# A layer normalisation that streams through SBUF: four instead of three rows of the fourth tile loaded one by one on the ScalarE queue

## The chip, the cores and the metric

One core of one Trainium2 chip. The metric is the device time of one execution in microseconds (us), the median of several; lower is better. "Tile 3" is the fourth tile; tiles are counted from 0. A packet is what one of the core's 16 DMA engines moves at a time; in the traces a full tile is 128 packets of 32 KB, eight for each engine, and a single row 128 packets of 4 KB.

## The reference

```python
def setup_inputs():
    batch, seq, dim = 32, 512, 1024
    return {"x": np.random.randn(batch, seq, dim).astype(np.float32), "eps": 1e-5}

def reference(x, eps):
    mean = np.mean(x, axis=-1, keepdims=True)
    var = np.var(x, axis=-1, keepdims=True)
    return ((x - mean) / np.sqrt(var + eps)).astype(np.float32)
```

67.1 MB come in and 67.1 MB go out; nothing is reused.

## The kernel before

The 16384 rows are 17 tiles: 15 of 128x8 rows, one of 128x6 and one of 128x2. A ring of 48 rows per partition holds six tiles. The loads go out on the SyncE queue: six tiles at once, and then tile t+6 when the store of tile t has landed. VectorE takes the statistics, GpSimd combines them, ScalarE takes the root, normalises in place and issues the store. So the ScalarE queue holds the stores, and, ahead of them, the few row loads that the change is about.

```python
TILES = (8,) * 15 + (6, 2)
SLOT, SLOTS = 8, 6
HALVES = (4, 4)                       # tile 0 is loaded in two halves
EARLY, AHEAD = 3, 3                   # <- the change
# ...
    for k in range(AHEAD):            # rows 0..AHEAD-1 of tile 3, one DMA each
        load(nc.scalar, EARLY, k, 1, ahead)
    owner = {}
    for t, (K, row, at) in enumerate(plan):
        # ... waits for the stores that free the ring's rows
        if t == 0:
            load(nc.sync, t, 0, HALVES[0], landed[t])
            load(nc.sync, t, HALVES[0], HALVES[1], second)
            continue
        first = AHEAD if t == EARLY else 0
        dma = load(nc.sync, t, first, K - first, landed[t])
# ...
    def vector(t, arrived, turn):
        K, row, at = plan[t]
        if t == EARLY:
            nc.vector.wait_ge(ahead, 16 * AHEAD)
        statistics(at, K, landed[t], arrived)
        nc.vector.reciprocal(out=rstd[:, at : at + K], in_=std[:, at : at + K]
        )._wait_ge(rooted[t], turn).then_inc(inverse, 1)
# ... ScalarE, for each tile: the root, then each row, then the store
        for k in range(at, at + n):
            a = nc.scalar.activation(out=ring[:, k, :], in_=ring[:, k, :],
                func=AF.Identity, bias=nmr[:, k : k + 1], scale=rstd[:, k : k + 1],
            ).then_inc(act, 1)
            # ...
            nc.scalar.dma_start(out=rows_of(o2, row, K), in_=ring[:, at : at + K, :]
            )._wait_ge(act, row + K).then_inc(stored[t], 16)
```

Of the kernel before, what the change touches and what calls it, by code (L numbers as in the profile page):

```python
# [16 lines left out]
HALVES = (4, 4)  # L17


EARLY, AHEAD = 3, 3  # L20


@with_exitstack
# [270 lines left out]
```

## Time and profile before

| | before |
|---|---|
| time, median of 3 (lowest to highest) | 318.32 us (318.27 to 318.82) |
| span in the profile | 316.7 us |
| busy: VectorE, ScalarE, GpSimd | 50%, 48%, 14% |
| DMA engines | 90% or more in 38 of 40 slices |
| rate in the middle (90 to 265 us) | 433 GB/s |

The prediction shows the lines that carry this (in the timeline: start, length, engine, line, what). In the timeline of the kernel before (start, length, engine, line, what), the SyncE queue issues tile 7's load as soon as store 1 has landed, and VectorE starts as soon as tile 4 has:

```profile
72.90 19.70 SPq L102 DMA_DIRECT2D ring<-in_x_dram  x2
73.74 9.59 DVE L128 BATCH_NORM_STATS2 stats<-ring 128x6 f32<-128x512 f32 x16 [6.32 <-DMA ring<-in_x_dram]
...
305.72 0.34 ACTq L251 DMA_DIRECT2D out_dram<-ring  x1
```

Two merged issues stand in the first line; its start, 72.90, is the landing of store 1 to within a tenth of a us. The second says that tile 4 had landed at 73.74. The third is the issue of the last store.

### The profile page before, as it was taken

What the parts mean: (1) busy time and instruction counts of PE and PEld (TensorE: products, weight loads), DVE (VectorE), ACT (ScalarE), POOL (GpSimd) and SP (SyncE); (2) the same over time, 40 slices, a digit from 0 to 9 for tenths busy, and PEclk for the clock granted to TensorE, in tenths of its full rate; (3) what the DMA queues carried; (4) which work ended last, traced back from release to release, by engine and by line L of the source; (5) the groups of instructions that cost most, each with busy time, mean ns of one, the idle gap of its engine ahead of it and who ended that gap; (6) DMA issues with size and microseconds to landing.
All of it is one profiled execution on the core that took longest, in us unless ns stands there. A gap on an engine that the chain in (4) does not pass through costs nothing.

```text
span 316.7 us, 712 instructions
## 1 busy us (share of the span) xinstructions
DVE 157.0 (50%) x274; ACT 153.3 (48%) x147; POOL 43.6 (14%) x186
## 2 busy tenths in 40 slices
DVE  0656584916529074380934709256191652918300
ACT  1065094947091561907429083380924709156740
POOL 0151202020200202001020110202002020021300
DMA  7999999999999999999999999999999999999996
GB/s 288 440 447 414 397 430 430 445 418 447 426 439 423 439 435 430 439 430 435 426 435 430 447 414 447 426 439 435 435 426 435 426 435 435 444 412 429 449 419 261
DMA packets 5476, 134.25 MB, mean 424 GB/s; under 512 B 608, under 2 KB 608, under 8 KB 992
## 3 DMA queue, kind: packets, MB, share of 16 engines
q10 hardware_dynamic: 2880, 68.68, 50.4%
q1 hardware_dynamic: 2592, 65.54, 48.5%
q14 instruction: 4, 0.03, 0.0%
HBM read 67.11 MB, written 67.11 MB: 424 GB/s over the span
## 4 chain that ended last, share of the span: by engine, by line
DVE 43%; another core or an unknown queue 23%; DMA 12%; POOL 10%; ACT 4%; issue 4%; SPq 0%; ACTq 0%; DVEq 0%
DVE stats L128 42%; DMA ring<-in_x_dram 12%; ACT ring L240 3%; ACT std L232 1%; POOL dev L193 1%; POOL dev L198 1%; POOL dev L186 1%; POOL nmean L182 1%; POOL dev L191 1%; POOL half L176 1%; POOL half L199 1%; POOL nmean L180 1%; POOL ss L202 1%; DVE rstd L141 1%
## 5 line engine op out<-in xcount | busy, mean ns | idle before, releaser
L128 DVE BATCH_NORM_STATS2 stats<-ring 128x6 f32<-128x512 f32 x256 | 153.7, 678 | 92.7 <-DMA ring<-in_x_dram 92.7
L240 ACT ACTIVATE ring<-ring,nmr,rstd 128x1024 f32<-128x1024 f32 x128 | 146.8, 1226 | 11.7 <-POOL nmr L223 11.7
L232 ACT ACTIVATE std<-ss,eps_t 128x8 f32<-128x8 f32 (+3 forms) x18 | 5.4, 299 | 138.4 <-POOL ss L202 138.0
L176 POOL TENSOR_TENSOR half<-stats 128x16 f32<-128x16 f32 (+3 forms) x18 | 4.1, 230 | 235.4 <-DVE stats L128 235.4
L141 DVE RECIPROCAL rstd<-std 128x8 f32<-128x8 f32 (+2 forms) x16 | 3.2, 200 | 52.3 <-ACT std L232 52.3
L193 POOL TENSOR_SCALAR dev<-dev 128x32 f32<-128x32 f32 (+3 forms) x18 | 5.1, 281 | 1.6
L223 POOL TENSOR_TENSOR nmr<-nmean,rstd 128x8 f32<-128x8 f32 (+3 forms) x18 | 3.7, 205 | 11.4 <-DVE rstd L141 11.3
L198 POOL TENSOR_TENSOR dev<-dev,stats 128x32 f32<-128x32 f32 (+3 forms) x18 | 4.5, 252 | 1.5
L182 POOL TENSOR_SCALAR nmean<-nmean 128x8 f32<-128x8 f32 (+3 forms) x18 | 4.3, 238 | 1.6
L186 POOL TENSOR_TENSOR dev<-stats,nmean 128x32 f32<-128x32 f32 (+3 forms) x18 | 4.3, 238 | 1.5
L191 POOL TENSOR_TENSOR dev<-dev 128x32 f32<-128x32 f32 (+3 forms) x18 | 4.2, 235 | 1.4
L199 POOL TENSOR_TENSOR half<-dev 128x16 f32<-128x16 f32 (+3 forms) x18 | 3.8, 213 | 1.4
L180 POOL TENSOR_TENSOR nmean<-half 128x8 f32<-128x8 f32 (+3 forms) x18 | 3.6, 203 | 1.4
L202 POOL TENSOR_TENSOR ss<-half 128x8 f32<-128x8 f32 (+3 forms) x18 | 3.6, 202 | 1.4
L232 ACT ACT_TABLE_LOAD x1 | 1.3, 1283 | 2.3 <-issue 2.3
L212 POOL TENSOR_TENSOR rstd<-std,power 128x4 f32<-128x4 f32 x2 | 2.1, 1040 | 0.9 <-ACT std L232 0.9
L145 DVE MEMSET eps_t<- 128x1 f32 x1 | 0.1, 59 | 1.0 <-SPq L56 1.0
L275 POOL MEMSET const-float32-0.0<- 128x1 f32 x1 | 0.1, 99 | 0.2 <-issue 0.2
L275 POOL MEMSET const-uint8-127<- 128x1 uint8 x1 | 0.1, 103 | 0.0
L275 POOL MEMSET const-bfloat16-1.0<- 128x1 bf16 x1 | 0.1, 102 | 0.0
L275 POOL MEMSET const-float32-1.0<- 128x1 f32 x1 | 0.1, 99 | 0.0
L146 DVE MEMSET power<- 128x8 f32 x1 | 0.1, 65 | 0.0
## 6 DMA issues: line engine op xcount, KB each, us to landing
out_dram<-ring ACTq DMA_DIRECT2D x15, 4096.0 KB, 34.6
ring<-in_x_dram SPq DMA_DIRECT2D x13, 4096.0 KB, 58.9
ring<-in_x_dram SPq DMA_DIRECT2D x2, 2048.0 KB, 11.4
ring<-in_x_dram SPq DMA_DIRECT2D x1, 3072.0 KB, 56.5
out_dram<-ring ACTq DMA_DIRECT2D x1, 3072.0 KB, 10.3
ring<-in_x_dram SPq DMA_DIRECT2D x1, 2560.0 KB, 51.5
ring<-in_x_dram ACTq DMA_DIRECT2D x3, 512.0 KB, 14.5
ring<-in_x_dram SPq DMA_DIRECT2D x1, 1024.0 KB, 68.3
```

Of the source, the lines that this page charges most:

```text
L128: i = nc.vector.bn_stats(out=stats[:, k, s, :], in_=ring[:, k, s * BN_MAX : (s + 1) * BN_MAX],)
L176: g.tensor_tensor(out=h, in0=mean4[:, :, 0:2], in1=mean4[:, :, 2:4], op=ALU.add),
L180: n = gp(g.tensor_tensor(out=nm, in0=h[:, :, 0], in1=h[:, :, 1], op=ALU.add), *n)
L182: g.tensor_scalar(out=nm, in0=nm, scalar1=-1.0 / H, scalar2=None, op0=ALU.mult),
L186: g.tensor_tensor(out=d, in0=mean4, in1=nm.unsqueeze(2).to_broadcast([P, K, H]), op=ALU.add),
L191: n = gp(g.tensor_mul(out=d, in0=d, in1=d), *n)
L193: g.tensor_scalar(out=d, in0=d, scalar1=float(D // H), scalar2=None, op0=ALU.mult),
L198: n = gp(g.tensor_tensor(out=d, in0=d, in1=m2, op=ALU.add), *n)
L199: n = gp(g.tensor_tensor(out=h, in0=d[:, :, 0:2], in1=d[:, :, 2:4], op=ALU.add), *n)
L202: g.tensor_tensor(out=ss[:, at : at + K], in0=h[:, :, 0], in1=h[:, :, 1], op=ALU.add),
L232: nc.scalar.activation(out=std[:, at : at + n], in_=ss[:, at : at + n], func=AF.Sqrt, bias=eps_t[:], scale=1.0 / D,)._wait_ge(*summed[i]). ...
L240: a = nc.scalar.activation(out=ring[:, k, :], in_=ring[:, k, :], func=AF.Identity, bias=nmr[:, k : k + 1], scale=rstd[:, k : k + 1],).then ...
```

## The change

```diff
-EARLY, AHEAD = 3, 3
+EARLY, AHEAD = 3, 4
```

One more of tile 3's rows goes on the ScalarE queue at the start, in a DMA by itself, and one less in tile 3's load on the SyncE queue. The intent that the code suggests: to keep both queues busy until the first store is ready. Nothing else changes.

## The prediction

> **What bounds the kernel now.** I read the page's digits by slice first, then a table of stretches, then the timeline of the first 55 us and of the end, and at last the packet records of the trace (start, queue, size of each packet), counted by me where a view has only a sum. The page's two DMA lines:
>
> ```profile
> DMA  7999999999999999999999999999999999999996
> GB/s 288 440 447 414 397 430 430 445 418 447 426 439 423 439 435 430 439 430 435 426 435 430 447 414 447 426 439 435 435 426 435 426 435 435 444 412 429 449 419 261
> ```
>
> In 38 of the 40 slices the DMA engines are busy for 90% or more, while VectorE and ScalarE are busy for 50% and 48% of the span. The stretches (length, VectorE, ScalarE and GpSimd busy us with instruction counts, clock, DMA share, GB/s):
>
> ```profile
> 2.00:15.00 13.00, 4.84 (x8) 1.28 (x1) 0.47 (x3) 1.00 1.02 420
> 15.00:26.00 11.00, 4.85 (x8) 6.14 (x7) 5.92 (x20) 1.00 1.01 432
> 26.00:40.00 14.00, 9.79 (x17) 3.96 (x6) 2.35 (x10) 1.00 0.99 400
> 90.00:265.00 175.00, 88.15 (x153) 85.86 (x83) 21.00 (x90) 1.00 1.00 433
> 303.00:310.00 7.00, 0.01 (x1) 2.37 (x2) 0.20 (x1) 1.00 0.99 425
> 310.00:314.40 4.40, 0.00 (x0) 0.00 (x0) 0.00 (x0) 1.00 0.81 344
> 314.40:316.70 2.30, 0.00 (x0) 0.00 (x0) 0.00 (x0) 1.00 0.01 4
> ```
>
> From 2 us to 314.4 us the transfers never pause. At 433 GB/s the 134.22 MB read and written (67.11 each way, from the page) take 310.0 us. Add 2.0 us ahead of the first byte, 2.3 us after the last, and the stretches below 433: 0.4 us in 2 to 15 (13 x 13/433), 1.1 us in 26 to 40 (14 x 33/433), 0.9 us in 310 to 314.4 (4.4 x 89/433). That is 316.7 us, the span. The time reported is 1.7 us longer (318.44 us for the profiled execution). So the kernel is a constant amount of traffic at a constant rate. The chain of waits puts 42% on VectorE's statistics, but this is not the bound: each of them starts when a tile lands, and in between VectorE waits for DMA (92.7 us in all).
>
> The start, where the change sits:
>
> ```profile
> 0.90 1.39 ACTq L102 DMA_DIRECT2D ring<-in_x_dram  x3
> 9.44 4.84 DVE L128 BATCH_NORM_STATS2 stats<-ring 128x6 f32<-128x512 f32 x8 [8.33 <-DMA ring<-in_x_dram]
> 15.63 4.85 DVE L128 BATCH_NORM_STATS2 stats<-ring 128x6 f32<-128x512 f32 x8 [1.35 <-DMA ring<-in_x_dram]
> 26.60 9.59 DVE L128 BATCH_NORM_STATS2 stats<-ring 128x6 f32<-128x512 f32 x16 [6.12 <-DMA ring<-in_x_dram]
> 29.64 0.35 ACTq L251 DMA_DIRECT2D out_dram<-ring  x1
> 39.42 0.20 DVE L141 RECIPROCAL rstd<-std 128x8 f32<-128x8 f32 x1 [3.24 <-ACT std L232]
> 40.44 9.59 DVE L128 BATCH_NORM_STATS2 stats<-ring 128x6 f32<-128x512 f32 x16 [0.81 <-DMA ring<-in_x_dram]
> 54.39 0.70 DVE L128 BATCH_NORM_STATS2 stats<-ring 128x6 f32<-128x512 f32 x1 [0.93 <-DMA ring<-in_x_dram]
> ```
>
> The statistics start when tile 0's halves land (9.44, 15.63), then tile 1 (26.60), tile 2 (40.44), tile 3 (54.39). Tile 3 is the "fourth tile". The first store goes out at 29.64.
>
> **What the Trainium skill says.** First, "DMA: Bandwidth & Descriptors", section "Queues, rings and completion order": each DMA engine takes turns between the queues that have work, a packet at a time, and takes the descriptors of one queue in order. The packet records agree: each of tile 0's halves is 128 packets of 16 KB on the SyncE queue, and in the same time exactly one row's 128 packets of 4 KB go on the ScalarE queue (first row 2.8 to 9.0 us, second 9.2 to 15.1); the third goes beside tile 1's 128 packets of 32 KB (16.0 to 26.1). Second, same page, "Issuing engines are not separate DMA queues": both queues feed the same 16 engines, so a second queue saves issue time only. The trace agrees: by packet records it is 430.7 GB/s with both queues loading (15 to 26 us), 432.4 with the SyncE queue alone (26.5 to 30) and 433 with loads beside stores (90 to 265). Third, same page, "Where 436 GB/s comes from", gives a ceiling of 435.2 GB/s; 433 is next to it, so I expect no rate above it. Fourth, same page, "Why a DMA increments its semaphore by 16 and not by 1": transfers that share a semaphore are only known to have landed at the full count. The kernel waits for 16 times the number of rows, which becomes 64, so the change is sound.
>
> **The change part by part.**
> 1. Added: one row load on the ScalarE queue. Three take 1.39 us to issue from 0.90, so a fourth takes some 0.46 us. It delays ScalarE's table load (2.3 us) to about 2.8 us; ScalarE is first needed at 17.0 us. Off the path: 0.
> 2. Removed: one row from tile 3's load on the SyncE queue, 2.5 MB to 2.0 MB (20 KB packets become 16 KB). The bytes are the same in all: 0. The row's 128 packets of 4 KB move at about 159 ns each against 1213 ns for 32 KB: 25.8 against 27.0 GB/s an engine. Half a MB at 4% less is 0.05 us.
> 3. Moved: the fourth row comes after the third in the ScalarE queue, so it starts at 26 us, beside tile 2. The two halves and tile 1 land as before. Tile 2 is now 8 rounds per engine of 1.213 + 0.159 us = 11.0 us from about 25.8 us: its packets end near 36.8 us and it lands near 37.5. In the kernel before, it had the engines alone only until the first store's packets came at 33.7 us, and landed at 40.4.
> 4. The first store, issued at 29.64 as before, sits behind the fourth row in the same queue: its packets start near 36.8 us instead of 33.7. It then goes beside tile 3: 8 rounds of 1.213 + 0.627 us (32 KB and 16 KB) = 14.7 us, both done near 51.6 us. Before, the store's packets ended at 50.5 and tile 3's at 53.1. The store loses 1 us, tile 3 gains 1.5 us.
> 5. From there nothing is left. Store 1 depends on tile 1, which has not moved: issued at 49.1 us, first packet at 52.8 us in the kernel before, after a gap from 50.5 in which its queue was empty. The 1 us that store 0 loses falls into this gap. Tile 4 starts near 51.7 instead of 52.0, and store 1 at 52.8 as before, packet by packet beside it. So the loads are about 0.3 us ahead from there to the end, and the stores where they were.
> 6. VectorE: tile 2's statistics cannot start before the reciprocal of tile 1 is through (39.42 + 0.20), so they start at 39.6 instead of 40.4; tile 3's near 52.8 instead of 54.4. Both off the path.
> Sum: 0 issue, +0.05 packets, 0 total bytes, 0 to -0.3 at the loads' end, which doesn't shorten the traffic. The time stays 318.3 us.
>
> **The end.** Could earlier loads still help there? The last store is issued at 305.7 us and its first packet goes at 311.1, behind the store before it; that one is issued at 302.1 and moves from 303.7, right behind its own predecessor. So the stores left over cover the last tiles' computing, and the engines run to 314.4 us. A last tile that comes 0.3 us earlier waits longer in the queue.
>
> **The rivals.**
> (a) The dip at the first store goes. By packet records the rate is 285 to 290 GB/s in 32 to 34 us and under 420 in 34 to 36, which loses (2 x 146 + 46 + 16)/433 = 0.8 us; some load packets there take 1.8 to 2.2 us instead of 1.2. If it comes from the first store meeting a queue that was empty, a fourth row ahead of it may hide it: 317.5 us. For it: the dip sits right between issue (29.6) and first packet (33.7). Against: the first store has to come at some time; I expect the dip to move, at the same size.
> (b) Holding the stores back costs at the end: if all stores stayed 3 us late, the last 4 MB would end later, up to 321 us. Against: the engines never idle, so a late store is an early load, and the gap after store 0 takes up the delay.
> (c) The fourth row delays what the first statistics wait for: if the rows shared bandwidth in equal parts and not by turns, both halves would land up to 1.2 us later (0.52 MB at 433 GB/s). This would delay the first store by as much, and the traffic would go on: 318.3 us all the same.
> (d) The end has no room: store 15's first packet goes right behind store 14's last, so if the loads' end came later by x, the end would come later by up to x. I expect it earlier; at most +0.5 us, 318.8.
>
> **Range and chances.** The three runs lie within 0.55 us. The rivals that I can size reach from -0.8 to +0.5 us. The range for 8 in 10 is 317.6 to 319.1 us. Two per cent are 6.4 us; neither direction has a mechanism of that size while the engines run without a pause: 0.01 faster, 0.98 same, 0.01 slower.
>
> **What would show each step.** In the profile after: statistics at 9.4, 15.6 and 26.6 us as before (step 3); tile 2's at 39.6, released by the reciprocal and not by a load (3, 6); tile 3's near 52.8 (4); the first store issued at 29.6, its first packet near 36.8 (4); tile 4's statistics within 0.5 us of the 73.7 us of before, and the last store's issue within 0.5 us of 305.7 (5); 433 GB/s in 90 to 265 us and the traffic's end at 314.4. The prediction is wrong if the engines pause anywhere between 3 and 310 us, or if the rate in the middle changes: 1% of it is 3.1 us.

## The result, and the profile after

Ratios below are the mean time of one kernel's runs over that of the other's in the same rounds, so they are not quite the ratio of the medians quoted.

| | before | after |
|---|---|---|
| time, median (lowest to highest), 4 runs each | 318.56 (318.27 to 318.82) | 318.96 (318.71 to 319.04) |
| ratio, 95% interval | | 1.0011 (0.9994 to 1.0029) |
| repeated, 11 and 5 runs | 318.69 | 318.99; 1.0014 (1.0001 to 1.0027) |

The same time, if anything 0.3 to 0.4 us longer. The page's DMA lines of the changed kernel:

```profile
DMA  7999999999999999999999999999999999999995
GB/s 282 446 447 443 343 447 438 428 430 455 409 455 406 451 409 451 422 447 430 430 455 409 451 409 451 418 443 422 447 430 430 451 414 430 447 414 434 443 434 245
```

As full as before; only the weak slice has become one with 343 (31.7 to 39.6 us), where the kernel before had 397, after 414 in the slice ahead of it. The stretches, as in the prediction:

```profile
90.00:265.00 175.00, 88.16 (x153) 85.98 (x82) 20.99 (x90) 1.00 1.00 433
...
303.00:310.00 7.00, 0.00 (x0) 1.92 (x2) 0.00 (x0) 1.00 1.02 440
310.00:314.40 4.40, 0.00 (x0) 0.00 (x0) 0.00 (x0) 1.00 0.82 348
314.40:316.90 2.50, 0.00 (x0) 0.00 (x0) 0.00 (x0) 1.00 0.02 7
```

The middle has the same 433 GB/s, and the traffic ends where it did. The start and the end of the timeline after:

```profile
0.90 2.14 ACTq L102 DMA_DIRECT2D ring<-in_x_dram  x4
...
9.56 4.84 DVE L128 BATCH_NORM_STATS2 stats<-ring 128x6 f32<-128x512 f32 x8 [8.45 <-DMA ring<-in_x_dram]
15.73 4.85 DVE L128 BATCH_NORM_STATS2 stats<-ring 128x6 f32<-128x512 f32 x8 [1.33 <-DMA ring<-in_x_dram]
...
26.74 9.59 DVE L128 BATCH_NORM_STATS2 stats<-ring 128x6 f32<-128x512 f32 x16 [6.16 <-DMA ring<-in_x_dram]
29.77 0.35 ACTq L251 DMA_DIRECT2D out_dram<-ring  x1
39.57 0.20 DVE L141 RECIPROCAL rstd<-std 128x8 f32<-128x8 f32 x1 [3.24 <-ACT std L232]
39.69 9.54 DVE L128 BATCH_NORM_STATS2 stats<-ring 128x6 f32<-128x512 f32 x16
...
53.32 9.59 DVE L128 BATCH_NORM_STATS2 stats<-ring 128x6 f32<-128x512 f32 x16 [0.65 <-DMA ring<-in_x_dram]
...
304.95 0.34 ACTq L251 DMA_DIRECT2D out_dram<-ring  x1
```

Tile 0's halves and tile 1 come 0.1 us later, which is nothing. Tile 2's statistics start at 39.69 without a wait for a load behind them: the reciprocal held them. Tile 3's start at 53.32, 1.1 us earlier than before, and the last store is issued 0.8 us earlier. By the packet records the fourth row moves from 27.0 to 37.6 us, beside tile 2, and the first store's first packet goes at 38.3 us, where it went at 33.7. Not all of these differences need come from the change: the section on the lag returns to this.

### The profile page after: what moved, and what is told of

Its sections match the earlier page's. It is cut to its first block, busy times and chain, and to the rows that moved or that the text cites. A ratio compares the mean times of both kernels' runs of the same rounds, so it can differ in the third digit from the quotient of the medians.

```text
span 316.9 us, 713 instructions
## 1 busy us (share of the span) xinstructions
DVE 156.8 (49%) x274; ACT 153.3 (48%) x147; POOL 43.6 (14%) x186
## 4 chain that ended last, share of the span: by engine, by line
DVE 46%; another core or an unknown queue 23%; POOL 11%; DMA 8%; ACT 4%; issue 4%; SPq 0%; ACTq 0%; DVEq 0%
DVE stats L128 45%; DMA ring<-in_x_dram 8%; ACT ring L240 3%; ACT std L232 2%; POOL dev L193 1%; POOL dev L198 1%; POOL dev L186 1%; POOL nmean L182 1%; POOL dev L191 1%; POOL half L176 1%; POOL half L199 1%; POOL nmean L180 1%; POOL ss L202 1%; DVE rstd L141 1%
```

## The experiments

The prediction held, so the question was whether for its reasons. The theory: a constant amount of traffic at a constant rate, so that only pauses and a changed rate count, and a store that comes late is a load that comes early. Twelve runs are each of five rounds against the kernel before. One is the changed kernel again (the last line of the table above; 0 to 0.4 us slower was expected), and two have one execution more or less than five. Where packets are counted, it is from the packet records of the trace.

### No row ahead, and seven

```diff
-EARLY, AHEAD = 3, 4
+EARLY, AHEAD = 3, 0      # ahead0; and VectorE's wait for `ahead` only if AHEAD
+EARLY, AHEAD = 3, 7      # ahead7
```

> No row of tile 3 ahead; all on the SyncE queue. Theory (a constant amount of traffic without a pause): same time, 318.3 to 318.9 us; tile 0's halves land some 1.2 us earlier each (statistics near 8.3 and 13.3 us), tile 1 near 23, the first store is issued near 26.5; the dip of the rate sits at the first store, with the same size of 0.8 to 0.9 us. Rival 'each row ahead costs 0.15 to 0.3 us of the start': 317.7 to 318.1 us. Rival (d), no room at the end: the loads end up to 1 us later than with four rows, and the time is up to 0.5 us longer than before's.

Measured: 318.29 us (318.20 to 319.11), ratio to before 0.9992 (0.9978 to 1.0006). The statistics of the halves ran from 8.18 to 17.89 us without a gap, the second half having landed at 13.0. The first store was issued at 28.37 us, later than the 26.5 expected, which had followed the second half: ScalarE normalises the first half until 22.0 us and only then takes the second's root, so the issue goes by the first half, which came 1.3 us earlier than in the kernel before (8.18 and 9.44; 28.37 and 29.64). The loads' end and the last store (305.81 us) were where the kernel before had them.

> Seven rows of tile 3 ahead, on the ScalarE queue in front of the first store. By turns, a row goes beside each of tiles 1 to 5, so the first store's packets come after all six tiles' loads, near 61 us (38 with four rows), and tile 3's statistics start near 61 us (53 with four). Theory: a late store is an early load, the engines never pause, 318.4 to 319.5 us; the loads end tens of us before the end. Rival (b), a store held back is paid at the end: up to 23 us more, 330 to 342 us. Rival 'each row costs 0.15 to 0.3 us': 319.3 to 320.2 us.

Measured: 318.55 us (318.50 to 318.76), ratio 0.9993 (0.9979 to 1.0006). Tile 3, the middle and the last store's issue in this run:

```profile
63.41 9.59 DVE L128 BATCH_NORM_STATS2 stats<-ring 128x6 f32<-128x512 f32 x16 [10.74 <-DMA ring<-in_x_dram]
...
290.00 0.34 ACTq L251 DMA_DIRECT2D out_dram<-ring  x1
```

```profile
90.00:265.00 175.00, 96.95 (x169) 94.28 (x91) 23.15 (x100) 1.00 1.00 433
```

The first store's packets started at 61.3 us, 27.6 us later than in the kernel before, and it cost nothing: the loads had its place, the computing was over at 290 us, and the stores left over kept the engines at 433 GB/s. Rival (b) of the prediction, that a store held back is paid at the end, falls. The idea that each row costs 0.15 to 0.3 us finds no support: four rows more than in the kernel before would be 0.6 to 1.2 us, some 0.5 us was saved elsewhere (the dip, next), and the run was 0.2 us faster, with an interval from 0.7 us faster to 0.2 us slower. Only the low end of that price, some 0.1 us net, would still hide in this noise.

These runs also answer rival (a), on the dip at the first store. From 27 us to 72 us, the loss against 431 GB/s summed by half microseconds is 0.7 to 0.9 us in three profiles of the kernel before (two of them with additions at the end, see below), 1.0 to 1.2 in four of the changed one, 1.2 with no row ahead; with seven rows, where tile 5's load was just over when the first store began, it is 0.4 us, all of it thinly spread. The dip lies at 29.5 to 34 us with no row ahead, at 31.5 to 35.5 with three and at 35.5 to 39 with four, where the first store's packets start at 32.7, 33.7 and 38.3: it moves with the first store, as predicted, and begins 2 to 3 us ahead of its packets. It all but goes in the one run where that store meets no load. When tile 6's load then joined the running stores, at 76.7 us, nothing was lost (0.0 us from 72 to 100). Why it begins ahead of the packets, no run tells.

### The fourth row elsewhere

```diff
-    for k in range(AHEAD):            # row_sync: the first three only, and
+    for k in range(AHEAD - 1):
         load(nc.scalar, EARLY, k, 1, ahead)
# ... in the loop over the tiles:
+        if t == EARLY:                # ahead of tile 3's rest, on SyncE
+            load(nc.sync, EARLY, AHEAD - 1, 1, ahead)
```

> The fourth row is a load by itself, but on the SyncE queue right ahead of the rest of tile 3. Theory: what moved tile 2 and the first store is the place in the ScalarE queue alone: tile 2 lands at 40.4 and the first store's packets start near 33.7 us, as in the kernel before; 318.5 us. Rival: the split into one more transfer moves them: tile 2 at 37.4 and the first store near 38, as with four rows on the ScalarE queue.

Measured: 318.73 us (318.69 to 318.84), ratio 1.0000 (0.9986 to 1.0013). Tile 2's statistics started at 40.42 us, behind a load, and the first store's packets at 33.74, as in the kernel before:

```profile
40.42 9.59 DVE L130 BATCH_NORM_STATS2 stats<-ring 128x6 f32<-128x512 f32 x16 [0.70 <-DMA ring<-in_x_dram]
```

It is the place in the ScalarE queue that moves both, not the split.

```diff
+    load(nc.gpsimd, EARLY, AHEAD - 1, 1, fourth)   # row_gpsimd: a third queue
-    for k in range(AHEAD):
+    for k in range(AHEAD - 1):
         load(nc.scalar, EARLY, k, 1, ahead)
```

VectorE waits for the new semaphore too.

> The fourth row on GpSimd's queue, a third one. By turns of a packet it goes beside the first half: both halves and tile 1 land 1.2 us later than in the kernel before (statistics near 10.7, 16.9, 27.8 us), and so does the first store's issue, near 30.9. Theory: 318.5 us all the same. Rival: what delays the first statistics delays the end: 319.7 us.

Measured: 323.19 us (323.04 to 323.91), ratio 1.0143 (1.0126 to 1.0160). The arrivals came as expected, and the time did not:

```profile
10.53 4.84 DVE L130 BATCH_NORM_STATS2 stats<-ring 128x6 f32<-128x512 f32 x8 [9.41 <-DMA ring<-in_x_dram]
17.18 4.84 DVE L130 BATCH_NORM_STATS2 stats<-ring 128x6 f32<-128x512 f32 x8 [1.81 <-DMA ring<-in_x_dram]
28.01 9.59 DVE L130 BATCH_NORM_STATS2 stats<-ring 128x6 f32<-128x512 f32 x16 [5.99 <-DMA ring<-in_x_dram]
```

```profile
90.00:265.00 175.00, 88.15 (x153) 82.14 (x79) 20.83 (x90) 1.00 1.00 426
```

The halves and tile 1 are 1.1 to 1.6 us late, but the price is 4.5 us. Most of it is paid in the middle: 426 GB/s instead of 433, with the engines busy throughout (share 1.00), is 2.8 us in this stretch alone. Both theories of this run fail: the traffic is constant, its rate is not. In the packet records, around the end of every tile, load packets take up to 2.2 us instead of 1.213; 166 load packets between 60 and 265 us take over 1.3 us, where the kernel before has 1. And the 16 engines drift apart: the last store's 16 completions are spread over 3.9 us instead of 1.1.

### A tiny first store

```diff
             load(nc.sync, t, HALVES[0], HALVES[1], second)
+            nc.sync.dma_start(out=rows_of(o2, row, K)[:, 0, 0:SLOT], in_=power[:]
+            )._wait_ge(filled, 1).then_inc(warm, 16)
```

ScalarE waits for `warm` ahead of store 0, which writes the same bytes over.

> The changed kernel with a tiny first store (32 bytes in each of 128 partitions, written over later) on the SyncE queue behind tile 0's halves. If the dip of the rate belongs to the very first store of the program: it moves to about 15 us, and if its size goes with the store's, it all but goes, for 0.5 to 0.9 us less than the changed kernel. If it belongs to the first large store beside loads: the rate dips at 35 to 39 us as in the changed kernel, same time.

Measured: one run of 325.10 us, which is the profiled one; the other five, 330 to 337 us, are over 1.5% above it, and are not compared. Their granted clock is 1.00 like that of all others, so they may as well be this kernel's own times; only the 325.10 was profiled. The fast run alone: 1.020 against 318.69; there is no interval for it, and the time rests on one run. The dip stayed (a loss of 0.7 us from 27 to 72 us), and the middle was as in the run above: 425 GB/s, 143 slow load packets, a spread of 3.9 us at the end. Nothing was gained, but it showed the same slow middle without GpSimd's queue. What both had in common: store 1 was issued late (50.5 and 50.7 us, where the kernel before had 49.1), because tile 1 was, and its first packet came 2.4 us after that of tile 4's load. In all other kernels so far, with seven rows left aside, this lag was between 0 and 1.2 us. A load packet takes 1.213 us, so it is two load packets per engine against one or none.

### The lag by itself

```diff
+        if t == 1:                    # lag_store1, in the changed kernel
+            nc.scalar.activation(out=idle[:], in_=eps_t[:].to_broadcast([P, 1536]),
+                func=AF.Identity)._wait_ge(*summed[i])
```

> The changed kernel with one more ScalarE activation of 128x1536 (about 1.4 us) ahead of tile 1's normalising, so that store 1 is issued at 50.7 instead of 49.3 us and its packets follow tile 4's loads by 2.4 us (two load packets per engine) instead of 1.2 (one). In the run with the fourth row on GpSimd's queue and in the one with a tiny store this lag was 2.4 us, load packets took up to 2 us around every tile's end and the 16 engines drifted apart by 4 to 5 us. Theory 'it is the lag': the same here, 321 to 325 us. Rival 'it is the kind of the added transfer': 318.7 to 319.3 us, no slow packets in the middle. The first theory of a constant traffic at a constant rate says 319 us too.

Measured: 323.43 us (323.35 to 325.11), ratio 1.0155 (1.0138 to 1.0172). The issue of tile 7's load (store 1 landed), tile 4's statistics (tile 4 landed), and then the stretches:

```profile
74.73 20.92 SPq L103 DMA_DIRECT2D ring<-in_x_dram  x2
...
72.13 9.59 DVE L129 BATCH_NORM_STATS2 stats<-ring 128x6 f32<-128x512 f32 x16 [4.37 <-DMA ring<-in_x_dram]
```

```profile
90.00:265.00 175.00, 88.14 (x153) 81.71 (x79) 20.83 (x90) 1.00 1.00 425
...
303.00:310.00 7.00, 0.63 (x2) 6.08 (x7) 2.06 (x10) 1.00 0.92 396
```

Compare with the lines of before: there store 1 landed 0.8 us ahead of tile 4, here 2.6 us behind it. One activation of 1.48 us on ScalarE, some 280 us ahead of the end and with no transfer added, costs 4.4 us against the changed kernel (318.99). The rate is 425 GB/s in the middle, 142 load packets are slow, and at 303 to 310 us the engines' share is 0.92: by my reading some have run out of work, waiting for the last two stores (issued at 306.66 and 310.25), while others have not. The expectation's "4 to 5 us" of drift was too high: by the completions it is 3.9 in all three runs.

```diff
+        if i == 1:                    # gps_later: issued after the second half's work
+            load(nc.gpsimd, EARLY, AHEAD - 1, 1, fourth)
```

> The fourth row on GpSimd's queue again, but issued after the second half's GpSimd work, near 25 us, so that it goes beside tile 2 and leaves tile 0, tile 1 and the issue of store 1 (49.2 us) where they were in the kernel before; store 1's packets should follow tile 4's loads by 0.8 to 1.2 us. Theory 'it is the lag': 318.5 to 319.2 us. Rival 'a transfer on GpSimd's queue by itself makes the later packets slow': 322 to 324 us as in the earlier run.

Measured: 318.75 us (318.28 to 319.02), ratio 0.9996 (0.9981 to 1.0010). The same row on the same GpSimd queue, and this is its middle:

```profile
73.42 19.68 SPq L102 DMA_DIRECT2D ring<-in_x_dram  x2
...
74.43 9.59 DVE L129 BATCH_NORM_STATS2 stats<-ring 128x6 f32<-128x512 f32 x16 [6.24 <-DMA ring<-in_x_dram]
```

```profile
90.00:265.00 175.00, 88.13 (x153) 85.88 (x83) 20.82 (x90) 1.00 1.00 432
```

GpSimd's queue by itself was not the cause. What goes with the slow middle in all these runs is the lag, and lag_store1 sets it directly, by holding up tile 1's work on ScalarE and nothing else. By packet records, one profile for each kernel:

| run | tile 4's first load packet, us | store 1's first packet, us | lag | GB/s, 90 to 265 us | load packets over 1.3 us, 60 to 265 us | last store's spread, us | median, us |
|---|---|---|---|---|---|---|---|
| ahead0 | 52.1 | 52.1 | 0.0 | 433 | 1 | 1.1 | 318.29 |
| gps_later | 52.1 | 52.7 | 0.7 | 433 | 6 | 1.8 | 318.75 |
| before | 51.9 | 52.8 | 0.85 | 433 | 1 | 1.1 | 318.56 |
| row_sync | 52.0 | 53.2 | 1.2 | 433 | 4 | 1.4 | 318.73 |
| after | 52.2 | 53.4 | 1.2 | 433 | 1 | 1.0 | 318.96 |
| before_end3 (below) | 52.0 | 53.2 | 1.2 | 432 | 5 | 1.0 | 318.66 |
| warm_store | 52.0 | 54.4 | 2.4 | 425 | 143 | 3.9 | 325.10 (one run) |
| row_gpsimd | 52.1 | 54.5 | 2.4 | 426 | 166 | 3.9 | 323.19 |
| lag_store1 | 52.2 | 54.6 | 2.4 | 425 | 142 | 3.9 | 323.43 |

The line of before_end3 (from the section on the end, below) is the kernel before itself, but for one more buffer and an activation added some 290 us after the start. Its lag is 1.2 us where the first profile of the same code had 0.85 and that of before_late3 0.7; tile 4 was ready at 72.4 us instead of 73.7, and store 1 landed at 73.9 instead of 72.9. So the lag and the loads' lead differ between executions of one kernel by as much as between the kernel before and the changed one. The four profiles of the changed kernel all have 1.2.

Why load packets get slow at the tiles' ends when the loads lead by two packets, no run tells, and none lies between 1.2 and 2.4 us. It is not lead as such: with seven rows ahead a load goes beside a store of another tile, far out of step, at 433 GB/s.

### The end

```diff
+        if t == len(plan) - 2:        # late3: between tile 15's last row and its store
+            nc.scalar.activation(out=idle[:], in_=eps_t[:].to_broadcast([P, 3072]),
+                func=AF.Identity)
```

> The kernel before, with one more ScalarE activation of 128x3072 in front of the store of the last tile but one, so that it and the last store go out about 3.3 us later (305.4 and 309.0 instead of 302.1 and 305.7). In the trace of before, that store's first packet follows its issue by 1.6 us, right behind the store before it. Rival (d), no room at the end: 2 to 3.3 us slower. If the stores left over cover it: the same time.

> The same addition in the changed kernel, where that store is issued at 301.4 us and its first packet goes at 304.05, 2.7 us later. If there is a limit at the end, the changed kernel has some 0.8 to 1.1 us more room, so the addition costs it 0.8 to 1.1 us less than the kernel before. If the end is covered in both, the same time in both.

Measured: 318.39 us, ratio 0.9992 (0.9979 to 1.0004), and 318.98 us, ratio 1.0012 (0.9999 to 1.0025): no cost. But the experiment did not do what it was for. The store waits for the count of normalised rows and not for the activation in front of it, and so it was issued at 302.19 us, beside the added one (302.06 to 304.81). Only the last store moved, from 305.7 to 307.9 us. The last two put the activation ahead of tile 15's root, so that its rows come later:

```diff
+        if t == len(plan) - 2:        # end3: ahead of tile 15's root
+            nc.scalar.activation(out=idle[:], in_=eps_t[:].to_broadcast([P, 3072]),
+                func=AF.Identity)._wait_ge(*summed[i])
```

> The kernel before with a ScalarE activation of 128x3072 (2.75 us, as measured) ahead of the last tile but one's normalising, which really delays its store, from 302.1 to 304.9 us, and the last store to 308.5. The store in front of it ends near 304.7 us, and a store issued on an empty queue had its first packet 3.6 to 4.1 us later. Rival (d), no room at the end: a pause of up to 3 us, 1.5 to 2.8 us slower. If the end is covered: the same time.

> The same addition in the changed kernel: that store goes from 301.4 to 304.1 us. If there is a limit at the end, the changed kernel has 0.8 us more room and loses 0.8 us less than the kernel before with the same addition; if the end is covered, the same time in both.

Measured: 318.66 us, ratio 0.9998 (0.9984 to 1.0012), and 318.93 us, ratio 1.0005 (0.9991 to 1.0019). In the kernel before, the last store but one went at 303.44 us and not at the 304.9 expected, because its loads happened to run 1.3 us early in that profile (the table above). The two last stores of the changed kernel with it:

```profile
304.22 0.34 ACTq L256 DMA_DIRECT2D out_dram<-ring  x1
...
307.81 0.34 ACTq L256 DMA_DIRECT2D out_dram<-ring  x1
```

The last store but one is 2.9 us later than without, and the time is the same. Its first packet followed the issue by 0.84 us (305.06), where its predecessor's last packets ended at 305.2. So there is room at the end for a store 2.9 us late, and rival (d) falls. A claim of mine falls with it: that a store needs 3.6 to 4.1 us from issue to first packet, as stores 0 and 1 did beside loads.

## Why the prediction was right

1. **The bound.** "A constant amount of traffic at a constant rate": right for both kernels (433 GB/s in the middle, last packet at 314.4 and 314.7 us), and so was the sum. The changed kernel is 318.96 us where 318.3 was predicted, inside 317.6 to 319.1 but near its top. Of the 0.66 us, 0.24 is that the kernel before came out slower with its fourth run (318.56). The rest, 0.4 us, I can trace in part only: the dip is 0.1 to 0.2 us larger (1.0 to 1.2 us in four profiles against 0.7 to 0.9 in three). The last packet is 0.3 us later than in the first profile of the kernel before, but that one was a fast execution (318.44 us); its other two, with additions at the end, have 314.7 and 315.2. A fixed price per row of 0.4 us is excluded by the run with seven; what makes up the rest stays open.
2. **Part 1, the issue.** The fourth issue made the four take 2.14 us, 0.75 more, where 0.46 was said. Off the path, as said.
3. **Parts 3 and 4, the queue's order.** The fourth row went beside tile 2, and the first store came behind it. Row_sync shows that the place in the queue does it. The sizes: tile 2 landed at 37.9 us (37.5 said), the first store's packets went at 38.3 us (36.8 said) and ended at 52.6 (51.6 said), tile 3's statistics started at 53.3 (52.8 said). The row's rounds started at 27.0 us and not at 25.8, hence the 1 to 1.5 us. The 0.627 us that the sum takes for a 16 KB packet is 0.611 in the trace, which changes nothing (14.6 us instead of 14.7).
4. **Part 5, the gap.** Store 0 lost 2.1 us, not 1, and most of it fell into the gap ahead of store 1, whose first packet went at 53.4 us (52.8 before and said). The loads got 0.6 to 0.8 us ahead, not 0.3 (tile 4 at 73.1 instead of 73.7; the last store's issue at 304.95 instead of 305.72), a little outside the half microsecond that the prediction allowed. But that the change did this is not shown: row_sync, whose first store is where it was, has 73.0 and 304.86, and before_end3, the kernel before itself, has tile 4 at 72.4. The effect on the time, none, is right.
5. **Part 6 and the end.** Tile 2's statistics were held by the reciprocal, as said (39.69). The leftover stores cover the end with room: end3 pushed a store by 2.9 us at no cost.
6. **The rivals.** (a) is settled: the dip moved with its size. (b) falls with ahead7, (d) with end3. But what the prediction says under (c) is wrong as a general claim: that the halves could land up to 1.2 us later and "the traffic would go on: 318.3 us all the same". It did not happen in this change, but where I made it happen (row_gpsimd), it cost 4.5 us. The step that failed is that the rate is constant whatever the order: with the loads two packets per engine ahead of the stores the middle runs at 425 to 426 GB/s, and the engines end 3.9 us apart. The changed kernel's lag of 1.2 us is one load packet short of that; the kernel before has 0.7 to 1.2. The prediction names a changed rate as a sign of being wrong, but no way to it is on its list, so in this it was right by luck. Its chance of 0.01 for "slower" was too sure, though the loss of 1.5% would still have been inside two per cent. Its range also leaves out what it grants to (b), up to 321 us.

## What to carry to other kernels

Where transfers run without a pause, as in this kernel, look for what a reordering of loads could buy in two places only: does a pause appear or go, and does the rate change? Here none of seven orders was faster than the kernel before. Read the rate in the middle before anything else. The order at the start sets how far the loads lead the stores, and this can persist to the end: here one short instruction on an idle engine cost 4.4 us. Before a difference of half a microsecond between two profiles is put down to a change, look at a second profile of the same kernel. When a change at the start moves the end by more than its own size, compare the landings of load and store at one tile, and the spread of the engines' completions, before blaming the new instruction.

## What the Trainium skill lacked or had wrong

- "DMA: Bandwidth & Descriptors", section "Queues, rings and completion order": it says that queues take turns by packets. It lacks that the share of the bytes then goes by packet size: beside 16 KB packets a queue of 4 KB packets got a fifth (128 of each from 2 to 9 us), beside 32 KB packets a ninth. And it lacks that the phase between a load and a store queue can change the rate: 432 to 433 GB/s with a lag of up to 1.2 us between the first packets of tile 4's load and of store 1, 425 to 426 with 2.4 us, and the last completions 3.9 us apart instead of 1.0 to 1.8.
- "DMA: Bandwidth & Descriptors", section "Issuing engines are not separate DMA queues": it says that issuing from several engines only saves issue time. It also changes the order: behind one more row on its queue the first store started at 38.3 us instead of 33.7.
- The same page, section "Latency and other measured facts", gives some 0.6 us to the first byte for these queues. Here it was 1.0 us for the first load (0.93 to 1.93), at most 0.84 us for a late store without loads beside it (the last packets of the store before it were still going), and 4.1 us for the first store, on an empty queue beside loads (29.6 to 33.7).
- The same page, section "Where 436 GB/s comes from", says that between HBM and SBUF some 358 GB/s bind. Taken by itself this misleads for a core that runs alone: here it was 433 GB/s of loads and stores for 175 us. The same section sets a measurement of 425 GB/s beside it.
- No page has the loss at the first store beside running loads: 0.7 to 1.2 us, once, and 0.4 us where it met no load.
